# Lower recurrence levels as pinned 32x32 blocks, and another order of the first loads, in a two-layer hybrid decoder block

## The chip, the core and the metric

The kernel runs on one core of one Trainium2 chip. The metric is the device time of one execution in microseconds (us). Before the change it is 418.7 us, the median of three runs (418.44 to 418.85).

## What is computed

Two layers of a decoder trunk over 256 tokens of width 1024, in float32. Cut to what matters here:

```
for l in range(2):
    h = rms_norm(x)                       # 256 x 1024
    q_a,k_a,v_a, q_h,f_h,i_h, q_m, z = split(h @ w_in[l])   # 1024 x 5120
    o_a = moba_attention(rope(norm(q_a)), rope(norm(k_a)), v_a)   # 8 heads x 64, causal
    o_h = hgrn2(q_h, f_h, i_h)            # 4 heads x 128, gated linear recurrence
    k_m, v_m = split(rms_norm(mem) @ w_mem_kv[l])           # 1024 x 1024
    o_m = memory_attention(q_m, norm(k_m), v_m)             # 4 heads x 128
    x = x + (concat(o_a, o_h, o_m) * silu(z)) @ w_out[l]    # 1536 x 1024
```

The recurrence (`hgrn2`) has a decay between every two tokens t >= s that is a product of forget gates: score(t, s) = sum over d of q[t,d] * F[s+1..t, d] * k[s,d], and o = scores @ i.

## The kernel before

**The weight stream.** All weights come as 120 tiles of 128x1024 float32 (512 KB each), in one fixed order per layer: 8 of `w_mem_kv`, then the ten column groups of `w_in` (FH, QH, IH, KA, QA, ZH, ZA, ZM, QM, VA, four tiles each), then 12 of `w_out`. SyncE issues each tile's load into one of four buffers `wr`. ScalarE (ACT) rounds a tile to the matmul format, `wh` (L144, or L147 where the norm's gain is folded in, three buffers); VectorE (DVE) forms the rest `wl` = `wr` - `wh` (L156 or L159, three buffers). TensorE (PE) then makes three products for each part of the result (high by high, high by low, low by high), each collected in `acc`, four banks of PSUM. `group_kv`, `group_b` and `group_a` (L198 to L290) are these loops for the three layouts, `w_out_phase` (L1082) that of the output projection, where `part` issues the products of one weight tile and `both` those of the last two tiles for one quarter of the result; in layer 1 `both` is called with `pinned=True`.

**Side work.** Everything else is written as Python generators (`g_norm`, `g_mem_r`, `g_hgrn`, `g_qk`, `g_moba_unit` and others). After each half or whole weight tile, `slot` lets each active generator take one step (`step`); a `yield n` skips n - 1 turns. They use four further PSUM banks `sd` (`side_tile`, counted by `room` and `rel`). A scheduler then orders each engine's instructions; `tc.keep_in_program_order` pins an instruction behind the pinned one before it on the same engine. All matmuls but those go through `mm` (L196), which doesn't pin.

**The recurrence.** `g_hgrn` (L710 to L856) works on `Q`, `K`, `F` of 128 partitions (head dimension) by 8x128 columns (4 heads, two halves of the tokens), and fills the score tile `hST`. It goes through levels m = 0, 1, 2, 4, 8, 16, 32, 64: at level m, keys of the lower half of each run of 2m tokens meet queries of its upper half, and afterwards `Q` and `K` are multiplied by the gates `Tm` over m tokens.
- m = 0, 1, 2 are sums over partitions: a product `pr` on DVE, split into `prh` and `prl`, then a matmul by a matrix of ones for each (`column_sums`, five 512-column results per layer).
- m = 4, 8, 16 are eight products of 128x128 each in float32 (all pairs of a half), of which a mask `mk` keeps the right ones: two DVE `copy_predicated` into `hST` for each level (`keep`, L723).
- m = 32 and 64 are the needed blocks alone: sixteen 32x32 or eight 64x64 blocks, copied by ACT into `hST` (L812).
- The product between the two halves of the tokens (`xc`, four 128x128) and the outputs follow.

A matmul with float32 operands leaves two records in the trace (two passes), those of the weight stream one.

**The start.** SyncE's queue carries `gT`, the transposed `mem`, weight tiles 0 to 3, then both halves of `x` (`xs`, 512 KB each), then weight tiles 4 to 7, then `mem` (`memr`). `g_norm(0)` takes the squares of `x` on ACT (L387) and scales on DVE; `g_mem_r` squares `memr` on ACT (L370), pinned, once the first layer's `hT` is there.

Of the kernel before, what the change touches and what calls it, by code (L numbers as in the profile page):

```python
# [45 lines left out]
def hymba_kernel(ctx: ExitStack, tc: tile.TileContext, x, mem, mem_t, positions, w_in, w_out, w_mem_kv,  # L46
# [256 lines left out]
    for t in range(2):  # L303
        load(xs[:, t], dram(x, t * 128 * D, [[D, 128], [1, D]]))
    dma_to(8)
# [20 lines left out]
    onesf = sb.tile([128, 128], F32, name="onesf", tag="sg", bufs=2)  # L326
    nc.gpsimd.memset(onesf, 1.0)
    ones = cst.tile([128, 128], F32R, name="ones")
    nc.vector.tensor_copy(ones, onesf)
# [92 lines left out]
    mk = cst.tile([128, 7, 128], U8, name="mk")  # L422
# [7 lines left out]
    def g_setup():  # L430
# [56 lines left out]
        for l in range(DEPTH):  # L487
            for q in range(2):
# [4 lines left out]
                def gb(a, n):  # L493
# [11 lines left out]
        oi = small("oi", 1)  # L505
        nc.vector.tensor_scalar(oi.bitcast(I32), si, 1, None, op0=OP.bitwise_and)
        od = small("od", 1)
        nc.vector.tensor_copy(od, oi.bitcast(I32))
        ti = sb.tile([128, 128], I32, name="ti", tag="sg", bufs=2)
        nc.gpsimd.iota(ti, pattern=[[1, 128]], base=0, channel_multiplier=0)  # L510
        xi = sb.tile([128, 128], I32, name="xi", tag="sg", bufs=2)
        xf = sb.tile([128, 128], F32, name="xf", tag="sq", bufs=2)
        xu = sb.tile([128, 128], F32, name="xu", tag="sq", bufs=2)
        nc.vector.tensor_tensor(xi, ti, si.to_broadcast([128, 128]), op=OP.bitwise_xor)
        nc.gpsimd.tensor_copy(xf, xi)
        nc.gpsimd.affine_select(xu, xf, pattern=[[1, 128]], compare_op=OP.is_ge, fill=-1.0, base=0,
                                channel_multiplier=-1)
        yield
        for j, m in enumerate((0, 1, 2, None, 4, 8, 16)):
            if m is not None:  # L520
                nc.gpsimd.tensor_scalar(mk[:, j], xu, float(m), None, op0=OP.is_ge)  # L521
        nc.gpsimd.tensor_tensor(xu, xu, od.to_broadcast([128, 128]), op=OP.mult)
        nc.gpsimd.tensor_scalar(mk[:, 3], xu, 2.0, None, op0=OP.is_ge)
# [186 lines left out]
    def g_hgrn(l):  # L710
# [7 lines left out]
        def keep(g, j, cols=slice(0, 128)):  # L718
            view = St[:, :, cols]
            n = view.shape[2]  # L720
            per = 512 // n
            for b in range(len(g)):
                nc.vector.copy_predicated(view[:, b * per:(b + 1) * per],  # L723
                                          mk[:, j, cols][:, None, :].to_broadcast([128, per, n]),
                                          g[b].rearrange("p (a s) -> p a s", s=n))
            rel("sd", len(g))

        def column_sums(n, make):
            yield from take("P", "PTh", "PTl")
            pr = sb.tile([128, n], F32, name="pr", tag="P", bufs=2)  # L730
            prh = sb.tile([128, n], F32R, name="prh", tag="PTh", bufs=1)
            prl = sb.tile([128, n], F32R, name="prl", tag="PTl", bufs=1)
            make(pr)
            nc.scalar.copy(prh, pr)
            nc.vector.tensor_tensor(prl, pr, prh.bitcast(F32), op=OP.subtract)
            yield 2
            yield from room("sd", n // 512)
            for b in range(n // 512):
                o = side_tile()
                mm(o, ones, prh[:, b * 512:(b + 1) * 512], True, False)  # L740
                mm(o, ones, prl[:, b * 512:(b + 1) * 512], False, True)
                res.append(o)
            for w in ("P", "PTh", "PTl"):
                rel(w)
            yield
# [6 lines left out]
        while m < 128:  # L752
            yield 2
            res = []
# [4 lines left out]
            if m == 0:  # L759
                yield from column_sums(1024, lambda o: nc.vector.tensor_tensor(o, Q, K, op=OP.mult))  # L760
                nc.vector.tensor_tensor(Q, Q, F, op=OP.mult)
                keep(res, 0)
                m = 1
                continue
            if m == 1:
                yield from column_sums(512, lambda o: nc.vector.tensor_tensor(o, Qv[:, :, 1, 0], Kv[:, :, 0, 0],
                                                                              op=OP.mult))
            elif m == 2:

                def make(o):  # L770
                    for j in range(2):
                        nc.vector.tensor_tensor(o[:, j * 512:(j + 1) * 512].rearrange("p (n i) -> p n i", i=2),
                                                Qv[:, :, 1], Kv[:, :, 0, j:j + 1].to_broadcast([128, 256, 2]),
                                                op=OP.mult)
                yield from column_sums(1024, make)
            elif m < 32:
                yield from room("sd", 2)
                for b in range(2):
                    g = side_tile()
                    for i in range(4):  # L780
                        c = slice((b * 4 + i) * 128, (b * 4 + i + 1) * 128)
                        mm(g[:, i * 128:(i + 1) * 128], K[:, c], Q[:, c], True, True)
                    res.append(g)
            else:
                yield from room("sd", 1)
                g = side_tile()
                res.append(g)
                for i in range(8):
                    for q in range(0, 128, 2 * m):
                        c = i * 128 + q  # L790
                        mm(g[q:q + m, i * m:(i + 1) * m], K[:, c:c + m], Q[:, c + m:c + 2 * m], True, True)
            yield 2
            nc.vector.tensor_tensor(Qv[:, :, 1], Qv[:, :, 1], Tv[:, :, 0:1].to_broadcast([128, n, m]), op=OP.mult)
            nc.vector.tensor_tensor(Kv[:, :, 0], Kv[:, :, 0], Tv[:, :, 1:2].to_broadcast([128, n, m]), op=OP.mult)
            if m < 64:
                T2 = sb.tile([128, n], F32, name=f"hT{m}", tag=f"hT{m}", bufs=1)
                nc.vector.tensor_tensor(T2, Tv[:, :, 0], Tv[:, :, 1], op=OP.mult)
                Tm = T2
            if m == 1:
                keep(res, 1, slice(1, 128, 2))  # L800
            elif m == 2:
                for j in range(2):
                    nc.vector.copy_predicated(
                        St.rearrange("p a (n r) -> p a n r", r=4)[:, :, :, 2:4],
                        mk[:, 2 + j].rearrange("p (n r) -> p n r", r=4)[:, None, :, 2:4].to_broadcast([128, 8, 32, 2]),
                        res[j].rearrange("p (a n i) -> p a n i", a=8, i=2))
                rel("sd", 2)
            elif m < 32:
                keep(res, int(math.log2(m)) + 2)
            else:  # L810
                for q in range(0, 128, 2 * m):
                    nc.scalar.copy(St[q:q + m, :, q + m:q + 2 * m],  # L812
                                   res[0][q:q + m, 0:8 * m].rearrange("p (a s) -> p a s", s=m))
                rel()
            m *= 2
# [91 lines left out]
    def g_moba_unit(l, u):  # L907
# [9 lines left out]
        for t in range(2):  # L917
            nk = 128 * (t + 1)
            yield from room("sd", 2)
            ps = [side_tile() for _ in range(2)]  # L920
            for i in range(4):
                pi, e = divmod(i, 2)
                mm(ps[e][:, pi * nk:(pi + 1) * nk], qT[64 * e:64 * e + 64, 2 * u + pi, t * 128:(t + 1) * 128],
                   kT[64 * e:64 * e + 64, 2 * u + pi, 0:nk], True, True)
# [157 lines left out]
    def w_out_phase(l):  # L1082
# [64 lines left out]
    spawn(g_mem_r(), 6)  # L1147
# [64 lines left out]
```

## Time and profile before

| | us |
|---|---|
| median of three runs (range) | 418.7 (418.44 to 418.85) |
| the profiled execution | 418.65 |
| its span, first to last instruction | 416.9 |
| outside the span | 1.75 |
| PE busy | 410.4 |
| DVE busy | 327.9 |
| ACT busy | 256.7 |
| POOL (GpSimd) busy | 58.5 |

The profile is that of one execution. A timeline row gives the start and the length of a run of like instructions, engine, line, operation, result and operands, shape, and their count; brackets at its end give the engine's idle time just before and what ended it. PE's matmuls overlap (the next one starts before the last has ended), so what a matmul costs is the distance from its start to the start of the next.

### The profile page before, as it was taken

The page shows a single profiled execution, that of the slowest core. Times are in us where ns is not written, and L with a number is a line of the kernel's source. Part 1 is how long each engine was busy: PE and PEld are TensorE (multiplying, and loading weights), DVE is VectorE, ACT ScalarE, POOL GpSimd, SP SyncE. Part 2 cuts the span into 40 slices and gives each one's busy share as a digit, 9 for nine tenths or more (in the row PEclk, how much of TensorE's full clock was granted, in tenths as well). Part 3 has the DMA queues.
Part 4 walks back from the last instruction along what each step waited for, and adds up shares of the span by engine and source line. Part 5 has one row for each costly group of instructions (what it writes and reads, how often), then busy time and mean ns, then how long its engine had stood idle before and what let it go on. Part 6 is the DMA issues. An engine that isn't in the chain of part 4 may idle for free.

```text
span 416.9 us, 6337 instructions
## 1 busy us (share of the span) xinstructions
PE 410.4 (98%) x2288; PEld 344.9 (83%) x2288; DVE 327.9 (79%) x617; ACT 256.7 (62%) x419; POOL 58.5 (14%) x78
## 2 busy tenths in 40 slices
PE   8999999999999999999999999999999999999996
PEld 6788888888878888888878888888888898888885
DVE  4789799999788984695568689899978797646854
ACT  5868766544579766664357676644454994748440
POOL 2006309046000021000000020003130002100000
PEclk9999999999999999999999999999999999999999
DMA  7984565555441654354546555555444144641602
GB/s 256 413 298 149 162 198 162 163 182 169 138 144 61 200 154 151 102 151 130 173 151 204 171 183 174 180 175 167 162 153 153 58 145 151 204 151 50 201 5 101
DMA packets 19616, 67.68 MB, mean 162 GB/s; under 512 B 2432, under 2 KB 2816, under 8 KB 19584
## 3 DMA queue, kind: packets, MB, share of 16 engines
q1 hardware_dynamic: 19296, 67.12, 48.9%
q8 instruction: 18, 0.29, 0.3%
q10 hardware_dynamic: 288, 0.15, 0.1%
q14 instruction: 14, 0.11, 0.1%
HBM read 66.22 MB, written 1.05 MB: 161 GB/s over the span
## 4 chain that ended last, share of the span: by engine, by line
PE 88%; DVE 4%; DMA 3%; POOL 2%; ACT 1%; issue 1%; SPq 0%; DVEq 0%
PE acc L196 56%; PE acc L1096 15%; PE sd L196 12%; DMA wr<-in_w_mem_kv_dram 3%; PE sd L960 1%; DVE wl L156 1%; POOL mk L521 1%; PE sd L1059 1%; DVE wl L159 1%; PE sd L403 1%; PE sd L899 1%; ACT wh L147 1%; DVE xs L1130 0%; PE sd L698 0%; PE sd L1005 0%
## 5 line engine op out<-in xcount | busy, mean ns | idle before, releaser
L144 ACT CAST wh<-wr 128x1024 fp32r<-128x1024 f32 x104 | 109.0, 1051 | 84.0 <-PE acc L196 62.5
L156 DVE TENSOR_TENSOR wl<-wr,wh 128x1024 fp32r<-128x1024 f32 x104 | 126.8, 1223 | 32.8 <-ACT wh L144 32.2
L196 PE MATMUL acc<-wh,hT 128*128 128x512 f32 x384 | 123.0, 394 | 0.0
L196 PE MATMUL acc<-hT,wh 128*128 128x512 f32 x256 | 91.8, 399 | 0.2 <-DVE vml L593 0.2
L196 PEld LDWEIGHTS acc<-wh,hT 128*128 128x128 f32 x384 | 71.9, 188 | 14.5 <-ACT wh L144 0.4
L196 PE MATMUL acc<-wl,hT 128*128 128x512 f32 x192 | 76.3, 398 | 0.0
L196 PE MATMUL acc<-hT,wl 128*128 128x256 f32 x256 | 72.4, 283 | 0.1
L196 PEld LDWEIGHTS acc<-hT,wh 128*128 128x128 f32 x256 | 48.0, 188 | 12.5 <-ACT wh L144 0.7
L196 PEld LDWEIGHTS acc<-hT,wl 128*128 128x128 f32 x256 | 48.3, 189 | 0.7 <-DVE wl L156 0.4
L196 PEld LDWEIGHTS acc<-wl,hT 128*128 128x128 f32 x192 | 36.2, 188 | 6.6
L1096 PE MATMUL acc<-wh,yl 128*128 128x512 f32 (+1 forms) x96 | 36.1, 391 | 0.0
L1096 PE MATMUL acc<-wl,yh 128*128 128x512 f32 (+1 forms) x96 | 36.0, 390 | 0.0
L1096 PE MATMUL acc<-wh,yh 128*128 128x512 f32 (+1 forms) x96 | 35.5, 393 | 0.0
L196 PE MATMUL acc<-wh,mTh 128*128 128x512 f32 x64 | 25.5, 399 | 1.6 <-ACT wh L147 1.1
L159 DVE SCALAR_TENSOR_TENSOR wl<-wr,gT,wh 128x1024 fp32r<-128x1024 f32 (+1 forms) x17 | 20.2, 1219 | 8.3 <-ACT wh L147 8.1
L147 ACT ACTIVATE wh<-wr,gT 128x1024 fp32r<-128x1024 f32 (+1 forms) x17 | 18.4, 1100 | 11.9 <-PE acc L1096 4.8
L196 PE MATMUL acc<-wh,mTl 128*128 128x512 f32 x64 | 25.0, 390 | 0.0
L1096 PEld LDWEIGHTS acc<-wh,yl 128*128 128x128 f32 x96 | 18.1, 188 | 3.8
L1096 PEld LDWEIGHTS acc<-wl,yh 128*128 128x128 f32 x96 | 18.1, 188 | 3.7
L1096 PEld LDWEIGHTS acc<-wh,yh 128*128 128x128 f32 x96 | 18.1, 188 | 3.6
L196 PE MATMUL acc<-wl,mTh 128*128 128x512 f32 x64 | 20.8, 393 | 0.2 <-DVE wl L159 0.2
L196 PEld LDWEIGHTS sd<-hQ,hK 128*128 128x128 f32 (+2 forms) x208 | 17.5, 159 | 1.9 <-DVE mxa L929 0.5
(215 smaller groups left out, 630.2 us busy)
## 6 DMA issues: line engine op xcount, KB each, us to landing
wr<-in_w_in_dram SPq DMA_DIRECT2D x80, 512.0 KB, 3.3
wr<-in_w_out_dram SPq DMA_DIRECT2D x24, 512.0 KB, 3.4
wr<-in_w_mem_kv_dram SPq DMA_DIRECT2D x15, 512.0 KB, 3.9
xs<-in_x_dram SPq DMA_DIRECT2D x2, 512.0 KB, 8.9
memr<-in_mem_dram SPq DMA_DIRECT2D x2, 512.0 KB, 6.4
out_dram<-xs SPq DMA_DIRECT2D x3, 256.0 KB, 2.0
mraw<-in_mem_t_dram SPq DMA_DIRECT2D x2, 256.0 KB, 5.3
wr<-in_w_mem_kv_dram SPq DMA_DIRECT2D x2, 256.0 KB, 4.6
```

Source lines behind the costliest of these rows:

```text
L144: nc.scalar.copy(whs[i], raws[i])
L147: nc.scalar.activation(whs[i][:, sl], raws[i][:, sl], AF.Copy, scale=gT[:, g:g + 1])
L156: nc.vector.tensor_tensor(wls[i], raws[i], whs[i].bitcast(F32), op=OP.subtract)
L159: nc.vector.scalar_tensor_tensor(wls[i][:, sl], in0=raws[i][:, sl], scalar=gT[:, g:g + 1], in1=whs[i][:, sl].bitcast(F32), op0=OP.mult, op ...
L196: nc.tensor.matmul(o, lhsT=a, rhs=b, start=s, stop=e)
L403: ins = nc.tensor.transpose(pt[:, j * 256 + t * 128:j * 256 + (t + 1) * 128], xn[t][:, k * 128:(k + 1) * 128], ident)
L521: nc.gpsimd.tensor_scalar(mk[:, j], xu, float(m), None, op0=OP.is_ge)
L899: nc.tensor.transpose(pt[:, p * 128:(p + 1) * 128], kr[:, t, p * 128:(p + 1) * 128], ident)
L960: nc.tensor.transpose(pt[:, i * 128:(i + 1) * 128], P[:, i, bs], ident)
L1059: nc.tensor.transpose(pt[:, i * 256 + t * 128:i * 256 + (t + 1) * 128], P[:, t, i, b * 128:(b + 1) * 128], ident)
L1096: ins = nc.tensor.matmul(a, lhsT=y, rhs=wt[:, cs], start=n == (0 if to is None else nk - 2) and j == 0, stop=n == nk - 1 and j == 2)
```

## The change

**Recurrence.** Each of the levels 0, 1, 2, 4, 8, 16 becomes 32 products of 32x32 (8 groups i of 128 columns by 4 blocks j, j the inner loop), block j written to the partitions 32j to 32j+31 of one PSUM tile of 128x256. One masked DVE copy per level puts it into a compact tile `hSd` (128x8x32). After m = 16, four ACT copies put `hSd` on the diagonal blocks of `hST`. The column sums, the matrix of ones and the wide masks go; `mk` is 128x6x32. At m = 32 and 64 the blocks of two groups a and a+1 are written to different partitions of the result, and the ACT copies are four and two where they were two and one. All these matmuls go through the new `mm_row`, which pins them in program order on PE.

**Attention scores.** The products of `kT` and `qT` in `g_moba_unit` go through `mm_row` too, and there is a `yield` between the 128-wide ones and the 256-wide ones.

**Output projection.** `both` pins in layer 0 as well, so that the last two weight tiles finish one quarter of the result after another.

**Start.** The queue carries x's first half, weight tile 4 (the fifth), x's second half, weight tile 5 (the sixth), then 6, 7 and `mem`. `g_mem_r` waits for nothing, isn't pinned, and starts at the ninth slot.

```diff
+    def mm_row(o, a, b):
+        tc.keep_in_program_order(nc.tensor.matmul(o, lhsT=a, rhs=b, start=True, stop=True))
...
     for t in range(2):
         load(xs[:, t], dram(x, t * 128 * D, [[D, 128], [1, D]]))
+        dma_to(5 + t)
     dma_to(8)
...
     def g_mem_r():
-        while "hT0" not in done:
-            yield
         ss = small("ssm", 2)
         for t in range(2):
-            tc.keep_in_program_order(nc.scalar.activation(memr[t], memr[t], AF.Square, accum_out=ss[:, t:t + 1]))
+            nc.scalar.activation(memr[t], memr[t], AF.Square, accum_out=ss[:, t:t + 1])
...
-    mk = cst.tile([128, 7, 128], U8, name="mk")
+    mk = cst.tile([128, 6, 32], U8, name="mk")
+    hSd = cst.tile([128, 8, 32], F32, name="hSd")
...
         while m < 128:
             yield 2
-            res = []
+            yield from room("sd")
+            g = side_tile()
+            if m < 32:
+                for i in range(8):
+                    for j in range(4):
+                        c = slice(i * 128 + j * 32, i * 128 + j * 32 + 32)
+                        mm_row(g[j * 32:j * 32 + 32, i * 32:i * 32 + 32], K[:, c], Q[:, c])
+            else:
+                for a in range(0, 8, 2):
+                    for q in range(0, 128, 2 * m):
+                        for b in range(2):
+                            c = (a + b) * 128 + q
+                            mm_row(g[q + b * m:q + b * m + m, a // 2 * m:(a // 2 + 1) * m],
+                                   K[:, c:c + m], Q[:, c + m:c + 2 * m])
+            yield 2
...
-            elif m < 32:
-                yield from room("sd", 2)
-                for b in range(2):
-                    g = side_tile()
-                    for i in range(4):
-                        c = slice((b * 4 + i) * 128, (b * 4 + i + 1) * 128)
-                        mm(g[:, i * 128:(i + 1) * 128], K[:, c], Q[:, c], True, True)
-                    res.append(g)
...
+            if m < 32:
+                j = m.bit_length()
+                nc.vector.copy_predicated(hSd, mk[:, j][:, None, :].to_broadcast([128, 8, 32]),
+                                          g[:, 0:256].rearrange("p (a s) -> p a s", s=32))
...
+            if m == 16:
+                for q in range(0, 128, 32):
+                    nc.scalar.copy(hST.rearrange("p h t s -> p (h t) s")[q:q + 32, :, q:q + 32], hSd[q:q + 32])
+            m = 2 * m or 1
...
         for t in range(2):
             nk = 128 * (t + 1)
+            if t:
+                yield
             yield from room("sd", 2)
...
-                both(t, c, 0, 256 if split else 512, last)
+                both(t, c, 0, 256 if split else 512, True)
...
-    spawn(g_mem_r(), 6)
+    spawn(g_mem_r(), 9)
```

The first place where it moves instructions is PE in layer 0, at the recurrence's level m = 16 (`sd<-hQ,hK`; `acc` rows are the weight stream). Before:

```order
L196 MATMUL acc<-hT,wh 128x512
L196 MATMUL acc<-hT,wl 128x256
L196 MATMUL sd<-hQ,hK 128x128 x8
L196 MATMUL acc<-hT,wh 128x512
L196 MATMUL acc<-hT,wl 128x256
```

After (L200 is `mm_row`, L851 transposes the attention's keys `kr`):

```order
L196 MATMUL acc<-wl,hT 128x512
L196 MATMUL acc<-wh,hT 128x512 x2
L200 MATMUL sd<-hQ,hK 32x32 x32
L851 MATMUL sd<-ident,kr 128x128 x4
L196 MATMUL acc<-wl,hT 128x512
L196 MATMUL acc<-wh,hT 128x512 x2
```

Eight wide products have become 32 small ones, and the level has moved to an earlier weight group, right ahead of four transposes. The other five low levels look alike, each one burst of 32 with 20 to 31 matmuls of the weight stream between two of them.

The second place is PE in layer 0 at the first unit's 256-wide attention scores (`sd<-kT,qT`). Before:

```order
L196 MATMUL acc<-hT,wh 128x512
L196 MATMUL acc<-hT,wl 128x256
L196 MATMUL sd<-kT,qT 128x256 x4
L196 MATMUL acc<-hT,wh 128x512
L196 MATMUL acc<-hT,wl 128x256
```

After:

```order
L196 MATMUL acc<-hT,wl 128x256
L200 MATMUL sd<-kT,qT 128x256
L196 MATMUL acc<-hT,wh 128x512
L196 MATMUL acc<-hT,wl 128x256
L196 MATMUL acc<-hT,wh 128x512
L200 MATMUL sd<-kT,qT 128x256 x3
L196 MATMUL acc<-hT,wl 128x256
```

One of the four now stands alone, with three matmuls of the weight stream between it and the other three; in layer 1 it is the same.

The third place is ACT at the start of the program, where it makes `wh` of the first tiles, squares `x` (`xn`) and later `mem` (`memr`). Before:

```order
L147 ACTIVATE wh<-wr,gT 128x1024
L387 ACTIVATE xn,ssx<-xs 128x1024 x2
L147 ACTIVATE wh<-wr,gT 128x1024 x4
L411 ACTIVATE hT<-sd,gT 128x256 x5
L144 CAST wh<-wr 128x1024
```

After:

```order
L147 ACTIVATE wh<-wr,gT 128x1024
L386 ACTIVATE xn,ssx<-xs 128x1024
L147 ACTIVATE wh<-wr,gT 128x1024
L386 ACTIVATE xn,ssx<-xs 128x1024
L147 ACTIVATE wh<-wr,gT 128x1024 x3
L369 ACTIVATE memr,ssm<-memr 128x1024
L410 ACTIVATE hT<-sd,gT 128x256 x3
L369 ACTIVATE memr,ssm<-memr 128x1024
```

The fifth tile's `wh` now stands between the two squares of `x`, and the squares of `mem` come earlier. ACT also loads its function tables fifteen times where it did so eleven times, twice more in each layer.

More of the change, by code (lines that the diff above doesn't have):

```diff
@@ L325, in hymba_kernel @@
     make_identity(nc, ident)
[L326 to L329, printed above, removed]
     pw = cst.tile([128, 16], F32, name="pw")
@@ L504, in g_setup @@
                                 base=0, channel_multiplier=1)
[L505 to L514, printed above, removed]
+        nc.gpsimd.memset(hSd, 0.0)
+        sp = small("sp", 1)
+        nc.vector.tensor_scalar(sp.bitcast(I32), si, 31, None, op0=OP.bitwise_and)
+        ti = sb.tile([128, 32], I32, name="ti", tag="sg", bufs=2)
+        nc.gpsimd.iota(ti, pattern=[[1, 32]], base=0, channel_multiplier=0)
+        xi = sb.tile([128, 32], I32, name="xi", tag="sg", bufs=2)
+        xf = sb.tile([128, 32], F32, name="xf", tag="sq", bufs=2)
+        ge = sb.tile([128, 32], F32, name="ge", tag="sq", bufs=2)
+        nc.vector.tensor_tensor(xi, ti, sp.bitcast(I32).to_broadcast([128, 32]), op=OP.bitwise_xor)
         nc.gpsimd.tensor_copy(xf, xi)
-        nc.gpsimd.affine_select(xu, xf, pattern=[[1, 128]], compare_op=OP.is_ge, fill=-1.0, base=0,
-                                channel_multiplier=-1)
+        nc.vector.tensor_tensor(xi, ti, sp.bitcast(I32).to_broadcast([128, 32]), op=OP.subtract)
+        nc.gpsimd.tensor_copy(ge, xi)
         yield
[L519 to L523, printed above, removed]
+        nc.gpsimd.tensor_scalar(ge, ge, 0.0, None, op0=OP.is_ge)
+        nc.gpsimd.tensor_scalar(xf, xf, 1.0, None, op0=OP.add)
+        nc.gpsimd.tensor_tensor(xf, xf, ge, op=OP.mult)
+        for j, m in enumerate((0, 1, 2, 4, 8, 16)):
+            nc.gpsimd.tensor_scalar(mk[:, j], xf, float(m + 1), None, op0=OP.is_ge)
     setup = g_setup()
@@ L716, in g_hgrn @@
         St = hST.rearrange("p h t s -> p (h t) s")
[L718 to L745, printed above, removed]
         Tm = F
@@ L758, in g_hgrn @@
                 Tv = Tm.rearrange("p (n two) -> p n two", two=2)
-            if m == 0:
-                yield from column_sums(1024, lambda o: nc.vector.tensor_tensor(o, Q, K, op=OP.mult))
-                nc.vector.tensor_tensor(Q, Q, F, op=OP.mult)
[L762 to L775, printed above, removed]
-            elif m < 32:
-                yield from room("sd", 2)
-                for b in range(2):
-                    g = side_tile()
-                    for i in range(4):
-                        c = slice((b * 4 + i) * 128, (b * 4 + i + 1) * 128)
-                        mm(g[:, i * 128:(i + 1) * 128], K[:, c], Q[:, c], True, True)
-                    res.append(g)
-            else:
[L785 to L810, printed above, removed]
-                for q in range(0, 128, 2 * m):
-                    nc.scalar.copy(St[q:q + m, :, q + m:q + 2 * m],
-                                   res[0][q:q + m, 0:8 * m].rearrange("p (a s) -> p a s", s=m))
-                rel()
@@ L815, in g_hgrn @@
-            m *= 2
+                nc.vector.tensor_tensor(Qv[:, :, 1], Qv[:, :, 1], Tv[:, :, 0:1].to_broadcast([128, n, m]), op=OP.mult)
+                nc.vector.tensor_tensor(Kv[:, :, 0], Kv[:, :, 0], Tv[:, :, 1:2].to_broadcast([128, n, m]), op=OP.mult)
+                if m < 64:
+                    T2 = sb.tile([128, n], F32, name=f"hT{m}", tag=f"hT{m}", bufs=1)
+                    nc.vector.tensor_tensor(T2, Tv[:, :, 0], Tv[:, :, 1], op=OP.mult)
+                    Tm = T2
+            else:
+                nc.vector.tensor_tensor(Q, Q, F, op=OP.mult)
@@ new lines, in g_hgrn @@
+            if m < 32:
+                j = m.bit_length()
+                nc.vector.copy_predicated(hSd, mk[:, j][:, None, :].to_broadcast([128, 8, 32]),
+                                          g[:, 0:256].rearrange("p (a s) -> p a s", s=32))
+            else:
+                S2 = hST.rearrange("p h t s -> p (h t) s").rearrange("p (a b) s -> p a b s", b=2)
+                for q in range(0, 128, 2 * m):
+                    for b in range(2):
+                        nc.scalar.copy(S2[q:q + m, :, b, q + m:q + 2 * m],
+                                       g[q + b * m:q + b * m + m, 0:4 * m].rearrange("p (a s) -> p a s", s=m))
@@ L816, in g_hgrn @@
+            rel()
+            if m == 16:
+                for q in range(0, 128, 32):
+                    nc.scalar.copy(hST.rearrange("p h t s -> p (h t) s")[q:q + 32, :, q:q + 32], hSd[q:q + 32])
+            m = 2 * m or 1
         yield 3
@@ L921, in g_moba_unit @@
             for i in range(4):
-                pi, e = divmod(i, 2)
-                mm(ps[e][:, pi * nk:(pi + 1) * nk], qT[64 * e:64 * e + 64, 2 * u + pi, t * 128:(t + 1) * 128],
-                   kT[64 * e:64 * e + 64, 2 * u + pi, 0:nk], True, True)
+                pi, e = i // 2, i % 2
+                mm_row(ps[e][:, pi * nk:(pi + 1) * nk], qT[64 * e:64 * e + 64, 2 * u + pi, t * 128:(t + 1) * 128],
+                       kT[64 * e:64 * e + 64, 2 * u + pi, 0:nk])
             yield
```

## The prediction

> **What bounds the kernel now.** I read the page first, for the shares and the chain.
>
> ```profile
> span 416.9 us, 6337 instructions
> PE 410.4 (98%) x2288; PEld 344.9 (83%) x2288; DVE 327.9 (79%) x617; ACT 256.7 (62%) x419; POOL 58.5 (14%) x78
> PE 88%; DVE 4%; DMA 3%; POOL 2%; ACT 1%; issue 1%; SPq 0%; DVEq 0%
> GB/s 256 413 298 149 162 198 162 163 182 169 138 144 61 200 154 151 102 151 130 173 151 204 171 183 174 180 175 167 162 153 153 58 145 151 204 151 50 201 5 101
> ```
>
> TensorE is busy for 410.4 of 416.9 us and carries 88% of the chain that ended last. A cut on another engine is worth what it takes from a PE wait; a cut on PE is worth its whole length. Next I looked for a stage in which another engine is as full, among the tables of busy time by window (length, then sum and count for PE, PEld, DVE, ACT and POOL, then clock, DMA share and GB/s).
>
> ```profile
> 80.00:100.00 20.00, 20.00 (x104) 16.84 (x103) 20.00 (x38) 8.71 (x12) 6.48 (x4) 1.00 0.52 169
> ```
>
> In the recurrence's first levels DVE is full too, but PE is never idle there, so DVE isn't ahead of it. The change is thus to be costed by starts of PE's matmuls: in the timeline of PE I take the distance between the starts of the two `acc` matmuls around a piece of side work, less what that distance is without it.
>
> **The low levels, removed.** Timeline of PE around level m = 16, around an undisturbed stretch, and around two column sums of one 512-column result:
>
> ```profile
> 108.30 0.28 PE L196 MATMUL acc<-hT,wl 128*128 128x256 f32 x1
> 108.42 1.95 PE L196 MATMUL sd<-hQ,hK 128*128 128x128 f32 x16
> 110.12 0.47 PE L196 MATMUL acc<-hT,wh 128*128 128x512 f32 x1
> 110.43 0.28 PE L196 MATMUL acc<-hT,wl 128*128 128x256 f32 x1
> ...
> 117.52 0.40 PE L196 MATMUL acc<-hT,wh 128*128 128x512 f32 x1
> 117.75 0.28 PE L196 MATMUL acc<-hT,wl 128*128 128x256 f32 x1
> 117.87 0.39 PE L196 MATMUL acc<-hT,wh 128*128 128x512 f32 x1
> 118.19 0.70 PE L196 MATMUL sd<-hQ,hK 128*32 128x32 f32 x32
> 118.82 0.39 PE L196 MATMUL acc<-hT,wl 128*128 128x256 f32 x1
> 119.04 0.40 PE L196 MATMUL acc<-hT,wh 128*128 128x512 f32 x1
> ...
> 66.99 0.62 PE L196 MATMUL sd<-prh,ones 128*128 128x512 f32 x2
> 67.44 0.39 PE L196 MATMUL acc<-wl,hT 128*128 128x512 f32 x1
> ```
>
> A 512-wide matmul costs 0.23 (117.52 to 117.75), a 256-wide one 0.12 (117.75 to 117.87), the pair 0.35. Level 16 takes 2.13 (108.30 to 110.43) where the pair alone takes 0.35: 1.78 for eight products. By the code there are three such levels: 5.34 per layer. A column sum costs 0.45 / 2 = 0.225, and there are ten: 2.25 per layer. Removed: 7.59.
>
> **The low levels, added.** No row shows 32x32 blocks in four column groups, but m = 32 has them in two. Sixteen passes of 128 columns take 1.70 (108.42 to 110.12), 0.106 each, so 32 columns stream in 0.0266. Level m = 32 costs 1.17 (117.87 to 119.04) less 0.35 = 0.82. One after another its 32 passes would stream for 0.85, yet only 0.63 lies between 118.19 and 118.82: blocks written to different partitions overlap. With two at a time that is 16 slots of 0.0266 = 0.43, and 0.39 for getting into and out of the small form. The new level has 64 passes; its inner loop goes through four partition groups, so four at a time make 16 slots too: 0.82, six times 4.92. Bounds: with all entries and exits shared with the transposes beside them, 0.43 each; two at a time or one at a time are rivals below. I take 0.82, the row with the same number of slots.
>
> The Trainium skill, "TensorEngine Tiling (Array Packing)", section "Tiling Modes", lists four independent tiles for 128 rows by 32 columns and says that switching the mode drains the engine. The 0.39 agrees with the second; no run here shows four yet. Against the change speaks "TensorE: Matmul & The Clock Gate", section "Wait — 56ns, not 53.3ns?": starts come no closer than some 25 ns however small a matmul is, so 64 passes would take 1.60, an estimate, where my sum has 0.43. The row at 118.19 speaks against it: 32 passes in 0.63 are 19.7 ns each.
>
> **Levels 32 and 64, and the attention scores.**
>
> ```profile
> 126.41 0.40 PE L196 MATMUL acc<-hT,wh 128*128 128x512 f32 x1
> 128.04 0.39 PE L196 MATMUL acc<-hT,wh 128*128 128x512 f32 x1
> ...
> 115.10 0.28 PE L196 MATMUL acc<-hT,wl 128*128 128x256 f32 x1
> 116.71 0.28 PE L196 MATMUL acc<-hT,wl 128*128 128x256 f32 x1
> ```
>
> At m = 32 four groups now alternate instead of two: 8 slots, 0.21 + 0.39 = 0.60, saving 0.22. At m = 64, 1.63 - 0.35 = 1.28 is 16 passes one after another (16 x 0.053 = 0.85) and 0.43; two groups halve the first part: saving 0.42. The four 256-wide score products cost 1.61 - 0.35 = 1.26: eight passes would stream 8 x 0.2125 = 1.70, so they overlap in pairs (0.85) with 0.41 around. Of the first unit's four, one now stands alone and three follow: three pairs' time becomes two for the three, one for the single, so 0.42 more of streaming and a second entry of 0.41 to 0.42: 0.84 lost per layer. Between 0, if the single one hides, and 0.84 I take all, since no row shows such a matmul hidden.
>
> Per layer: 4.92 - 0.22 - 0.42 + 0.84 - 7.59 = -2.47; two layers **-4.94**. Bursts that now stand beside transposes may share an entry, 0.2 to 0.4 per layer more; that stays in the range.
>
> **The start.** Timelines of PE, ACT and DVE:
>
> ```profile
> 16.61 1.07 PE L196 MATMUL acc<-wl,mTh 128*128 128x512 f32 x4
> 18.00 0.50 PE L196 MATMUL acc<-wh,mTh 128*128 128x512 f32 x1 [0.31 <-ACT wh L147]
> 18.33 0.40 PE L196 MATMUL acc<-wh,mTl 128*128 128x512 f32 x1
> 19.71 0.39 PE L196 MATMUL acc<-wh,mTl 128*128 128x512 f32 x1
> 20.29 0.50 PE L196 MATMUL acc<-wl,mTh 128*128 128x512 f32 x1 [0.19 <-DVE wl L159]
> ```
>
> ```profile
> 12.95 1.15 ACT L147 ACTIVATE wh<-wr,gT 128x1024 fp32r<-128x1024 f32 x1 [0.22 <-DMA wr<-in_w_mem_kv_dram]
> 15.43 1.06 ACT L387 ACTIVATE xn<-xs 128x1024 f32<-128x1024 f32 x1
> 16.79 4.99 ACT L147 ACTIVATE wh<-wr,gT 128x1024 fp32r<-128x1024 f32 x4 [0.21 <-DVE msx L391]
> ```
>
> ```profile
> 18.96 4.87 DVE L159 SCALAR_TENSOR_TENSOR wl<-wr,gT,wh 128x1024 fp32r<-128x1024 f32 x4
> ```
>
> PE waits twice for the fifth tile. The four matmuls at 16.61 would end at 16.61 + 4 x 0.23 = 17.53 but the next starts at 18.00: 0.47, and it takes 0.33 instead of 0.23 after the pause: 0.10. At 19.71 + 0.23 = 19.94 the next should come and comes at 20.29: 0.35, and 0.10 more behind it. Together 1.02. The cause is the queue: at 413 GB/s (the page's second slice) 512 KB land every 1.27, tile 3 was used on landing at 12.95, and two halves of x lie between it and tile 4: 12.95 + 3 x 1.27 = 16.76, and ACT takes it at 16.79. With one half ahead it lands at 15.49, and its `wh` is ready 1.1 to 1.2 later, before 17.53. What is late next is x's second half and so tile 5's `wl` on DVE, behind the scaling of x: from x's square at 15.43 to that `wl` group at 18.96 are 3.53; from 16.76 they give 20.29, and 1.22 for one `wl` (4.87 / 4) gives 21.5. From 17.53 PE has twelve matmuls of tile 4 and eight of tile 5 with `wh` to do first, 20 x 0.23, so it is wanted at 22.1: 0.6 to spare. I take **-1.02**, between 0 (the pause moves to tile 5) and that.
>
> ```profile
> 36.85 0.28 PE L196 MATMUL acc<-hT,wl 128*128 128x256 f32 x1
> 37.37 0.50 PE L196 MATMUL acc<-hT,wh 128*128 128x512 f32 x1 [0.25 <-DVE vml L593]
> ...
> 210.55 0.40 PE L1096 MATMUL acc<-wh,yl 128*128 128x512 f32 x1
> 211.45 0.48 PE L196 MATMUL acc<-wh,mTh 128*128 128x512 f32 x1 [0.51 <-DVE xs L1130]
> 211.76 0.40 PE L196 MATMUL acc<-wh,mTl 128*128 128x512 f32 x1
> ```
>
> At 36.85 + 0.12 PE waits 0.40 for `vml` to free a bank, and pays 0.10 behind it. `mem`'s squares, on which `vml`'s factor hangs, now come before `hT`. Between 0 and 0.50 I take **-0.3**, since other DVE work stands in between as well.
>
> **Between the layers.** All four `acc` banks of the output projection end together, so the next layer's first matmul waits for their addition into `xs`: 211.45 - 210.55 - 0.23 = 0.67, and 211.76 - 211.45 - 0.23 = 0.08 behind it. Pinned, the quarters end one after another, each 1.4 (six matmuls of 0.23) before the next, and the first three additions are done by the end: **-0.75**. If the last addition were still waited for, 0.
>
> **New waits.** ACT gets two more table loads per layer and three more copies.
>
> ```profile
> 121.69 1.28 ACT L941 ACT_TABLE_LOAD   x1
> 133.19 1.05 ACT L144 CAST wh<-wr 128x1024 fp32r<-128x1024 f32 x1
> ...
> 135.66 0.48 PE L196 MATMUL acc<-hT,wh 128*128 128x512 f32 x1
> ```
>
> Two loads are 2.56 per layer. Queued behind them on ACT is the next `wh`, and PE waits for that. Where ACT's lead is shortest, `wh` is done at 133.19 + 1.05 = 134.24 and used at 135.66: 1.4 to spare. Both loads in one such place cost 2.56 - 1.4 = 1.14 per layer, spread out nothing; I take 0.4, nearer to nothing as one load fits into the lead: **+0.8** for both layers.
>
> **DVE.** One of the masked copies that go:
>
> ```profile
> L723 DVE COPY_PREDICATED hST<-mk,sd 128x512 f32<-128x512 uint8 x18 | 14.1, 796 | 0.0
> ```
>
> DVE loses 14.1 us of these, and the column sums' products, for six copies of half the width per layer. I cost that at zero: PE hides it, as the 80 to 100 us window shows. It is also why pinned levels should not wait: the update of Q and K between two levels had two such copies beside it and now has one of half the size.
>
> **Sum.** -4.94 - 1.02 - 0.3 - 0.75 + 0.8 = -6.2 against the profiled 418.65 (416.9 and 1.75 outside), which stands 0.05 under the median: **412.4 us**.
>
> **Rivals.** *Two at a time.* PE runs only pairs, as in all the rows: a level has 32 slots, between 32 x 0.0266 + 0.39 = 1.24 and twice 0.63 plus the remaining 0.19 = 1.45; at 1.33, six are 7.98, m = 32 saves nothing, and a layer comes to 7.98 - 0.42 + 0.84 - 7.59 = +0.81. With the other terms (-1.27) that is +0.35: 419.0. For it: pairs are all that is shown. Against: nothing shows a limit at two. Chance 0.12.
>
> *One at a time, slower.* The new level's blocks write all of a PSUM tile's partitions in turn and don't overlap at all: 64 x 0.0266 + 0.39 = 2.09, six 12.54, m = 32 and m = 64 as before, +0.84 - 7.59: +5.8 per layer, so 418.65 + 11.6 - 1.3 = 429. It decides once a level costs more than 1.23, where 6 x 1.23 + 0.84 - 7.59 eats the other terms' 0.64 per layer. Against it stands the row at 118.19. Chance 0.04. The skill's 25 ns would make a level 1.99 and the time near 428, an estimate; it is counted here.
>
> *New waits eat a part.* Table loads at their full 1.14 or more per layer, or a pinned level that waits for DVE while the weight stream stands behind it (20 to 31 matmuls, 4.6 to 7.1 us, lie between two levels): 1.5 to 4 more, 414 to 416.5. For it: the DVE window is full, and a pinned matmul can't be passed by a later pinned one. Chance 0.14.
>
> **How the numbers follow.** My forecast, 409.8 to 414 (shared entries -1.6, the unknown terms +1.6), has 0.68; the waits 0.14; two at a time 0.12; one at a time 0.04; 0.02 is left for faster still. The range 409.8 to 416.8 holds the first two. About 0.2%, 0.84 us, is what a measurement of this kernel can tell from no change: faster has the first, the waits and the rest with part of two at a time, 0.86; within it lies most of two at a time, 0.08; slower 0.06.
>
> **What would show it.** Right: level bursts of 64 records with 0.6 to 0.7 us between the start of the first and the next `acc` matmul; no pause at 17.5 and 20 us; a first matmul of layer 1 without a wait for `xs`. Wrong: bursts of 1.2 (pairs) or 2 us (single file), a lone `kT` matmul costing nothing, new brackets on PE naming ACT `wh` or DVE `hQ`.

## The result, and the profile after

| | before | after |
|---|---|---|
| median, us | 418.66 | 411.12 (410.86 to 411.35) |
| the profiled execution's span | 416.9 | 409.6 |
| PE busy | 410.4 | 404.7 |
| DVE busy | 327.9 | 305.6 |
| ACT busy | 256.7 | 261.7 |

The ratio after to before is 0.9816, 95% interval 0.9802 to 0.9831: 7.5 us faster, where 6.2 was forecast. The page of the changed kernel:

```profile
span 409.6 us, 7613 instructions
PE 404.7 (99%) x2940; PEld 336.7 (82%) x2940; DVE 305.6 (75%) x592; ACT 261.7 (64%) x431; POOL 54.5 (13%) x79
PE 97%; DMA 1%; DVE 0%; SPq 0%; ACT 0%; issue 0%; DVEq 0%
```

PE's share of the chain has gone from 88% to 97%: almost no wait for another engine is left in it. PE's busy time fell by 5.7 and the span by 7.3; the other 1.6 is time in which PE stood idle before. Part of a wait counts as busy (the pause before 18.00 us in the kernel before is 0.47 by the starts and 0.31 in its bracket), so the distances of starts, below, give the better split.

**A low level.** Timeline of PE around the first one in layer 0 (start, length, instruction):

```profile
61.67 0.39 PE L196 MATMUL acc<-wh,hT 128*128 128x512 f32 x1
61.98 0.76 PE L200 MATMUL sd<-hQ,hK 128*32 128x32 f32 x64
62.68 0.51 PE L196 MATMUL acc<-wh,hT 128*128 128x512 f32 x1
63.02 0.39 PE L196 MATMUL acc<-wl,hT 128*128 128x512 f32 x1
```

From 61.67 to 63.02 are 1.35, less two undisturbed 512-wide matmuls (0.46): the level costs 0.89; 0.82 was forecast. The 64 passes take 0.70 from first start to the next `acc`, 10.9 ns each. In the single records of this burst the first starts of a round through the four groups lie 6 or 7 ns apart, and a whole round takes 32 ns.

**Level 64 and the attention scores.** The same view further on:

```profile
109.87 0.69 PE L200 MATMUL sd<-hQ,hK 128*64 128x64 f32 x16
110.49 0.71 PE L200 MATMUL sd<-kT,qT 64*128 64x128 f32 x8
...
113.33 0.28 PE L196 MATMUL acc<-hT,wl 128*128 128x256 f32 x1
113.54 0.70 PE L200 MATMUL sd<-kT,qT 64*128 64x256 f32 x2
114.16 0.50 PE L196 MATMUL acc<-hT,wh 128*128 128x512 f32 x1
114.50 0.28 PE L196 MATMUL acc<-hT,wl 128*128 128x256 f32 x1
114.61 0.40 PE L196 MATMUL acc<-hT,wh 128*128 128x512 f32 x1
114.94 1.13 PE L200 MATMUL sd<-kT,qT 64*128 64x256 f32 x6
116.00 0.38 PE L196 MATMUL acc<-hT,wl 128*128 128x256 f32 x1
116.22 0.40 PE L196 MATMUL acc<-hT,wh 128*128 128x512 f32 x1
```

Level 64 takes 0.62 from its start to that of the scores and has no exit of its own, where before the whole level cost 1.28. The lone 256-wide score costs 114.50 - 113.33 - 0.35 = 0.82 (two records: one matmul), the other three 116.22 - 114.61 - 0.35 = 1.26: together 0.82 more than the four in one piece before.

**The start and the seam.** Timeline of PE at the start, and where layer 1's first matmuls on `hT` begin:

```profile
16.88 1.07 PE L196 MATMUL acc<-wl,mTh 128*128 128x512 f32 x4
17.79 0.39 PE L196 MATMUL acc<-wh,mTh 128*128 128x512 f32 x1
...
19.60 1.07 PE L196 MATMUL acc<-wl,mTh 128*128 128x512 f32 x4
20.51 0.39 PE L196 MATMUL acc<-wh,mTh 128*128 128x512 f32 x1
...
22.32 0.62 PE L196 MATMUL acc<-wl,mTh 128*128 128x512 f32 x2
...
229.79 0.39 PE L196 MATMUL acc<-wl,mTh 128*128 128x512 f32 x1
230.17 0.50 PE L196 MATMUL acc<-hT,wh 128*128 128x512 f32 x1
230.50 0.28 PE L196 MATMUL acc<-hT,wl 128*128 128x256 f32 x1
```

From 16.88 to 22.32 there are 24 matmuls, and each start follows the one before it by the undisturbed distance: 24 x 0.227 = 5.44. Neither pause is left. The wait between the layers has gone as well, but a new one of 230.17 - 229.79 - 0.23 = 0.15, and 0.10 behind it, stands at 230.

**Where the 7.3 us went.** I took the prediction's measure (starts of `acc` matmuls, less their undisturbed distance) over both whole traces. Side work on PE falls from 73.4 to 68.6: 4.84. Waits between two `acc` matmuls fall by 2.4, of which 2.3 can be named: at the start 1.03, for `vml` 0.51, near 52 and 64 us in layer 0 0.35 and 0.23, between the layers 0.75; against them 0.32 new at 7 us and 0.26 at 230. The first `acc` matmul started 0.11 earlier.

### The profile page after: what moved, and what is told of

Same layout as the page of the kernel before. It is cut to its first block, busy times and chain, and to the rows that moved or that the text cites. A ratio compares the mean times of both kernels' runs of the same rounds, so it can differ in the third digit from the quotient of the medians.

```text
span 409.6 us, 7613 instructions
## 1 busy us (share of the span) xinstructions
PE 404.7 (99%) x2940; PEld 336.7 (82%) x2940; DVE 305.6 (75%) x592; ACT 261.7 (64%) x431; POOL 54.5 (13%) x79
## 4 chain that ended last, share of the span: by engine, by line
PE 97%; DMA 1%; DVE 0%; SPq 0%; ACT 0%; issue 0%; DVEq 0%
PE acc L196 65%; PE acc L1050 16%; PE sd L196 6%; PE sd L200 4%; DMA wr<-in_w_mem_kv_dram 1%; PE sd L914 1%; PE sd L851 1%; PE sd L1013 1%; PE sd L402 1%; PE sd L698 0%; PE sd L959 0%; PE sd L578 0%; SPq L119 0%; ACT wh L147 0%; DVE xs L1084 0%; DVE xs L1091 0%
## 5 line engine op out<-in xcount | busy, mean ns | idle before, releaser
L1050 PE MATMUL acc<-wl,yh 128*128 128x512 f32 (+1 forms) x96 | 37.4, 389 | 0.0
L1050 PE MATMUL acc<-wh,yl 128*128 128x512 f32 (+1 forms) x96 | 37.1, 393 | 0.0
L1050 PE MATMUL acc<-wh,yh 128*128 128x512 f32 (+1 forms) x96 | 36.6, 392 | 0.0
L819 POOL TENSOR_TENSOR rka<-msa,pw 128x8 f32<-128x8 f32 x4 | 14.2, 3560 | 54.2 <-DVE msa L818 54.2
```

The costliest lines, as they stand in the source:

```text
L819: nc.gpsimd.tensor_tensor(r[:, t8], ms[:, t8], pw[:, :8], op=OP.pow)
L1050: ins = nc.tensor.matmul(a, lhsT=y, rhs=wt[:, cs], start=n == (0 if to is None else nk - 2) and j == 0, stop=n == nk - 1 and j == 2)
```

## The experiments

Times below are compared through the ratio to the kernel before, run in turn on the same chip (its median was 419.05 to 419.34 there).

**Single file.** Only the two loops change places:

```diff
-                for i in range(8):
-                    for j in range(4):
+                for j in range(4):
+                    for i in range(8):
```

> The changed kernel with the two loops of a low level swapped (block j outer, group i inner), so that eight blocks in a row go to the same partitions. Theory (blocks overlap because neighbours go to different column groups): 64 passes one after another at 31.6 ns, the spacing of the pairs at m = 32, are 2.02 us and 0.33 around them, 2.35 instead of the 0.89 that the changed kernel's bursts cost; 12 levels make +17.5, 428 to 430. Rival (the order within a burst doesn't matter, the gain comes from the fewer columns and from DVE's relief): 411 to 412. A floor of 25 ns from start to start whatever the group: 64 x 25 = 1.60 and 0.33, +12.5, near 424.

**Pairs.** The groups alternate in twos:

```diff
-                for i in range(8):
-                    for j in range(4):
+                for i, j in [(i, j + e) for j in (0, 2) for i in range(8) for e in range(2)]:
```

> The changed kernel with the low levels' blocks going through two partition groups at a time, first 0 and 1, then 2 and 3. Theory (as many overlap as there are groups in turn): 32 slots of 31.6 ns are 1.01, with 0.33 around 1.34 instead of 0.89; 12 levels +5.4, 416 to 417. Rival one (the engine overlaps two at most): no change from the changed kernel, 411. Rival two (order doesn't matter): 411 too; the single-file run tells these two apart.

Measured: 426.39, ratio 1.0178 (1.0155 to 1.0201), and 415.85, ratio 0.9927 (0.9905 to 0.9949). The same 32 products in another order turn a gain of 1.8% into a loss of 1.8%. Timeline of PE around one level, single file and then pairs:

```profile
72.42 0.39 PE L196 MATMUL acc<-wh,hT 128*128 128x512 f32 x1
72.74 1.91 PE L200 MATMUL sd<-hQ,hK 128*32 128x32 f32 x64
74.58 0.50 PE L196 MATMUL acc<-wh,hT 128*128 128x512 f32 x1
74.91 0.39 PE L196 MATMUL acc<-wl,hT 128*128 128x512 f32 x1
```

```profile
61.65 0.39 PE L196 MATMUL acc<-wh,hT 128*128 128x512 f32 x1
61.97 1.11 PE L200 MATMUL sd<-hQ,hK 128*32 128x32 f32 x64
63.01 0.50 PE L196 MATMUL acc<-wh,hT 128*128 128x512 f32 x1
63.34 0.39 PE L196 MATMUL acc<-wl,hT 128*128 128x512 f32 x1
```

A level costs 74.91 - 72.42 - 0.46 = 2.03 in single file, 63.34 - 61.65 - 0.46 = 1.23 in pairs and 0.89 in fours. The prediction's rivals had priced the first two at 2.09 and 1.33 (1.24 at the least). The expectation for single file, 2.35 at 31.6 ns a pass, was 0.32 too high for a level. In the single records 41 of the 63 distances in such a burst are 31 or 32 ns, as it took, but around each of the three changes of group some passes start 5 or 6 ns after the one before, which brings the mean down to (2.03 - 0.33) / 64 = 26.6. Over twelve levels that is 3.8 us; the time came out only some 2 us lower than expected, and the difference isn't traced. The number of column groups in turn sets the price, and two isn't the limit.

**Recurrence and score pins alone**, the start's loads, mem's squares and the output projection as before.

```diff
-        dma_to(5 + t)
-                both(t, c, 0, 256 if split else 512, True)
+                both(t, c, 0, 256 if split else 512, last)
-    spawn(g_mem_r(), 9)
+    spawn(g_mem_r(), 6)
```

(and `g_mem_r` waits for `hT0` and pins its squares again.)

> The changed kernel without its start order, with mem's squares as before and without the pinned quarters in layer 0: the recurrence and the attention pins alone. Theory (PE's side work is 4.84 us shorter in the changed kernel, and two waits of 0.35 and 0.23 in layer 0 that the prediction didn't count went with DVE's relief): 418.7 - 5.4 = 413.3, with the pauses at 17 and 20 us, the one for the bank of vml and the one between the layers still there. Rival (most of the gain is DVE's relief, the start and the seam): 416 or more.

**The rest alone**: the kernel before with the lines above as in the change.

```diff
+        dma_to(5 + t)
-                both(t, c, 0, 256 if split else 512, last)
+                both(t, c, 0, 256 if split else 512, True)
-    spawn(g_mem_r(), 6)
+    spawn(g_mem_r(), 9)
```

> The kernel before with the new start order, mem's squares as in the change and the pinned quarters in layer 0, and the old recurrence and attention. Theory (terms add): start -0.7 to -1.0, vml -0.5, seam -0.75: 416.4 to 416.8. Rival (the pauses only move, as DVE is as full as before): 418 or more.

Measured: 413.74, ratio 0.9871 (0.9856 to 0.9886), or 5.4 us, and 416.3, ratio 0.9939 (0.9917 to 0.9962), or 2.6. They add up to 8.0 where the change has 7.7 by its ratio, which agrees within the intervals. The parts aren't quite independent: the two waits near 52 and 64 us, 0.58 together, are gone from either run's trace and so stand in both numbers. The waits of PE in the first:

```profile
PE acc L196 <- DVE xs L1085: 0.5, 1, 0.5
PE acc L196 <- DVE vml L594: 0.3, 1, 0.3
```

The waits for `xs` between the layers and for `vml` are still there although DVE is as light as in the changed kernel, so DVE's relief didn't take them. Of the two pauses at the start, which were expected here too, this execution has only the second (0.26, and 0.11 behind it). Its first `acc` matmul starts at 6.99 us, where the kernel before has 6.51. With the old order of loads the two pauses come to 1.02, 0.37 and 1.26 in the three traces that have it (before, this run, the seam alone), so one execution doesn't fix what they cost.

**Seam alone**, the kernel before with `both(..., True)`.

```diff
-                both(t, c, 0, 256 if split else 512, last)
+                both(t, c, 0, 256 if split else 512, True)
```

> The kernel before with the last two weight tiles of layer 0's output projection pinned quarter by quarter, nothing else. Theory: the wait of 0.67 and the 0.08 behind it between the layers go, 418.7 - 0.75 = 417.9. Rival (the wait moves to the next tiles' wh or wl, whose buffers the last two tiles now hold to the end): 418.5 or more.

**Start alone**, the kernel before with the new order of loads.

```diff
         load(xs[:, t], dram(x, t * 128 * D, [[D, 128], [1, D]]))
+        dma_to(5 + t)
```

> The kernel before with the new order of the first loads, nothing else. Theory: both pauses for the fifth tile go, 418.7 - 1.0 = 417.7. Rival (the pause moves to tile six, whose wl stands behind x's scaling on DVE): 418.4 or more, with a new bracket near 21 us.

Measured: 418.46, ratio 0.9983 (0.9974 to 0.9991), 0.7 us or 0.4 to 1.1; and 417.0, ratio 0.9952 (0.994 to 0.9964), 2.0 us. The start is worth twice what I gave it. PE's waits in that run:

```profile
PE sd L196 <- DVE dm L319: 1.0, 1, 1.0
PE acc L196 <- ACT wh L147: 1.0, 1, 1.0
PE acc L196 <- DVE xs L1131: 0.5, 1, 0.5
```

What is left of waits are the very first matmuls (`dm`, `wh`) and the seam. The wait for `vml` has gone too, with mem's squares untouched, and so have the two near 52 and 64 us: with the pauses, 1.02 + 0.51 + 0.58 = 2.1, which is the measured gain. Of the last two the first shows in the kernel before as a distance:

```profile
52.25 0.39 PE L196 MATMUL acc<-hT,wh 128*128 128x512 f32 x1
52.72 0.39 PE L196 MATMUL acc<-hT,wl 128*128 128x256 f32 x1
```

52.25 to 52.72 is 0.47 where 0.23 is undisturbed. The row has no bracket naming what ended it. The recurrence-only run shows neither of the two distances either, so each part alone takes them away; which wait they were stays open.

**Mem's squares as before**, in the changed kernel.

```diff
+        while "hT0" not in done:
+            yield
-            nc.scalar.activation(memr[t], memr[t], AF.Square, accum_out=ss[:, t:t + 1])
+            tc.keep_in_program_order(nc.scalar.activation(memr[t], memr[t], AF.Square, accum_out=ss[:, t:t + 1]))
-    spawn(g_mem_r(), 9)
+    spawn(g_mem_r(), 6)
```

> The changed kernel with mem's squares as before (pinned on ACT, behind the first layer's hT, sixth slot). The prediction's step: the earlier squares free the bank that vml holds, so the wait of 0.40 and 0.10 behind it comes back near 37 us: 411.1 + 0.5 = 411.6. Rival (the start order alone took that wait away, since the kernel before with only the start order showed none of it): 411.1, no bracket naming vml.

Measured: 412.2, ratio 0.9842 (0.9825 to 0.986). PE's waits:

```profile
PE sd L196 <- DVE dm L323: 1.0, 1, 1.0
PE acc L196 <- ACT wh L147: 0.8, 1, 0.8
```

No wait for `vml` comes back. The ratio lies 0.3% above that of the change, with overlapping intervals; if that is a difference, it isn't this wait.

**Scores as before**, in the changed kernel.

```diff
-            if t:
-                yield
-                mm_row(ps[e][:, pi * nk:(pi + 1) * nk], qT[64 * e:64 * e + 64, 2 * u + pi, t * 128:(t + 1) * 128],
-                       kT[64 * e:64 * e + 64, 2 * u + pi, 0:nk])
+                mm(ps[e][:, pi * nk:(pi + 1) * nk], qT[64 * e:64 * e + 64, 2 * u + pi, t * 128:(t + 1) * 128],
+                   kT[64 * e:64 * e + 64, 2 * u + pi, 0:nk], True, True)
```

> The changed kernel with the attention scores as before: not pinned, no turn between the 128-wide and the 256-wide ones. The prediction priced pin and turn as a loss of 0.84 per layer. If that holds against this kernel too: 411.1 - 1.6 = 409.5. Rival (they avert something worse: in this kernel's order the unpinned 256-wide scores of both units stand two and two, both of one row group, which can't overlap): each half is four passes of 0.2125 and 0.41 around, 1.26, so 2.52 for a unit; first unit +0.44, second +1.26 per layer, 411.1 + 3.4 = 414.5.

Measured: 416.14, ratio 0.9943 (0.9921 to 0.9966): 1.3% above the change's ratio, some 5 us. Timeline of PE at the first unit's 256-wide scores:

```profile
114.01 0.28 PE L196 MATMUL acc<-hT,wl 128*128 128x256 f32 x1
114.22 1.13 PE L196 MATMUL sd<-kT,qT 64*128 64x256 f32 x4
115.61 0.28 PE L196 MATMUL acc<-hT,wl 128*128 128x256 f32 x1
```

Two matmuls (four records) cost 115.61 - 114.01 - 0.35 = 1.25, as much as four that alternate: both use the same row group (the same 64 of PE's 128 rows). A second such pair follows at 117.09, and the second unit is split likewise. From level 32 to the outputs' last matmul the side work costs 12.36 where the changed kernel's costs 10.68, so 3.4 for both layers, the rival's price. All side work is 4.6 longer; the remaining 1.2 has, among others, a wait for `wl` of 0.4 in each layer. So in the changed kernel's order pin and turn are a gain; against the kernel before, whose four stood together, they are a loss of 0.82, where the prediction gave 0.84.

**Scores whole**, first unit's 256-wide and the second unit later.

```diff
+        if u:
+            yield 2
...
             if t:
-                yield
+                yield 3 if u == 0 else 1
```

> The changed kernel with the first unit's 256-wide scores two turns later and the second unit two turns later, so that all four stand together in both units (beside the product between the halves and beside the outputs' first matmuls). Theory (a split costs an entry and the overlap, 0.82 per layer in the changed kernel's trace): 411.1 - 1.6 = 409.5. Rival (the later scores make softmax and its transposes late, and PE waits there, or nothing changes as the split is paid elsewhere): 411 or more.

Measured: 416.61, ratio 0.9938 (0.9925 to 0.9951), 5 us slower than the change. Timelines of ACT and PE:

```profile
137.24 0.49 ACT L897 ACTIVATE P<-P,nba,rq 128x128 f32<-128x128 f32 x1
...
141.42 0.19 ACT L897 ACTIVATION_READ_ACCUMULATOR P<-P,nba,rq 128x1 f32 x1
141.51 1.04 ACT L144 CAST wh<-wr 128x1024 fp32r<-128x1024 f32 x1
```

```profile
143.01 0.71 PE L196 MATMUL acc<-wh,hT 128*128 128x512 f32 x2
144.99 0.50 PE L196 MATMUL acc<-wl,hT 128*128 128x512 f32 x1 [1.27 <-DVE wl L156]
```

All scores stand whole, and the 0.82 per layer is there on PE. But eight exponentials of the second unit now stand in one piece on ACT (137.24 to 141.51) ahead of the next `wh`; its `wl` comes after, and PE waits 1.27, in both layers. These waits, with what stands behind them, are 3.1 of the 5 us. Later transposes and value products fall apart into more pieces: side work as a whole is 1.6 longer, although the scores are 1.6 shorter. This is the prediction's "new waits" rival, in an order in which it bites.

**Two milder orders.** One turn less before the first unit's wide scores and one more before the second's; and the first unit's as in the run above, with the second unit not delayed as a whole.

```diff
+        if u:
+            yield 2
...
             if t:
-                yield
+                yield 2
```

> The changed kernel with both units' 256-wide scores one turn later than in it and the second unit two turns later: all scores whole, as in the run with two turns, but three of the first unit's exponentials have a tile's wh between them and the rest on ACT. Theory (whole scores are worth 1.6 us, and what cost more there was wh behind the exponentials): with that wait away 409.5. Rival (the second unit's softmax is late in any case, and PE waits for a weight tile behind its exponentials): 411 or more, with a bracket of 1 us or so naming DVE wl or ACT wh near 143 us.

```diff
             if t:
-                yield
+                yield 3 if u == 0 else 2
```

> The changed kernel with the first unit's 256-wide scores two turns later (whole, beside the product between the halves) and the second unit's one turn later; of the second unit's 128-wide scores one then stands in that same burst and three apart. Theory (bursts alone): -0.82 for the whole scores, +0.2 for the one apart, per layer: 411.1 - 1.2 = 409.9. Rival (later scores, exponentials ahead of wh): 411 or more.

Measured: 411.83, ratio 0.9832 (0.9815 to 0.9848), and 411.7, ratio 0.9819 (0.9806 to 0.9833): neither can be told from the change. In the first, PE's timeline shows part of what gave the gain back, here in layer 0 and once more in layer 1:

```profile
145.03 0.38 PE L916 MATMUL sd<-ident,P 128*128 128x128 f32 x2
145.91 0.50 PE L196 MATMUL acc<-wl,hT 128*128 128x512 f32 x1 [0.50 <-DVE wl L156]
```

**Exponentials pinned**, on top of the first of these two.

```diff
-                nc.scalar.copy(whs[i], raws[i])
+                tc.keep_in_program_order(nc.scalar.copy(whs[i], raws[i]))
...
-                nc.scalar.activation(P[:, i, kc[t]], P[:, i, kc[t]], AF.Exp, bias=nb[:, c:c + 1],
-                                     scale=rq[:, r:r + 1], accum_out=sm[:, c:c + 1])
+                tc.keep_in_program_order(nc.scalar.activation(P[:, i, kc[t]], P[:, i, kc[t]], AF.Exp, bias=nb[:, c:c + 1],
+                                     scale=rq[:, r:r + 1], accum_out=sm[:, c:c + 1]))
```

(the gain-folding cast of `wh` is pinned likewise.)

> The kernel of the shorter whole scores with ACT's casts to wh and the attention's exponentials pinned in the order in which they are written, so that no more than four exponentials stand ahead of a wh; ACT then loads its tables seven times instead of fifteen. Theory (what whole scores gained was given back where wh stood behind eight exponentials): the wait for wl near 145 us goes; on PE alone the bursts are about 0.8 shorter than the changed kernel's: 0.2% below it, a ratio to the kernel before of 0.980. Rival (a pinned wh now stands behind exponentials that wait for their row maxima, and the weight stream stops): 412 or more, a ratio of 0.984 or more, with brackets naming ACT wh or DVE wl between 125 and 145 us.

Measured: 421.18, ratio 1.0047 (1.0033 to 1.0061). Both missed the place. Timelines of ACT and PE, and the busy time by window (columns as in the prediction's window row):

```profile
46.18 1.28 ACT L484 ACT_TABLE_LOAD   x1
49.97 0.23 ACT L484 ACTIVATE sc<-rt 128x32 f32<-128x32 f32 x1 [2.50 <-DVE rt L483]
50.10 2.92 ACT L144 CAST wh<-wr 128x1024 fp32r<-128x1024 f32 x3
```

```profile
51.19 0.79 PE L196 MATMUL acc<-hT,wh 128*128 128x512 f32 x1 [5.89 <-ACT wh L144]
...
162.39 0.50 PE L196 MATMUL acc<-wl,hT 128*128 128x512 f32 x1 [0.48 <-DVE wl L156]
```

```profile
40.00:44.00 4.00, 4.00 (x25) 3.52 (x24) 2.90 (x12) 2.87 (x6) 3.77 (x10) 1.00 0.39 132
...
51.19:55.30 4.11, 3.95 (x11) 2.95 (x12) 3.61 (x3) 1.84 (x2) 4.11 (x8) 0.50 0.41 135
```

Pinning moved three `wh` behind the sine of the position angles (L484), which waits for DVE; PE stood still for 5.89 us and then ran at half the clock for about 4. The wait that the pins were meant to remove is there too, later and in both layers (162.39): eight exponentials again stand in one piece on ACT (154.82 to 159.09) ahead of the next `wh`, not four. So what whole scores gain without that wait stays open.

## Why the prediction was right

Step by step, in us of the whole kernel:

- *Recurrence and scores*, -4.94 forecast, -4.84 measured on PE. The levels run four at a time, as taken, and the row of level 32 was the right one to price them by: 0.89 for 0.82. The split of that price was off: 16 rounds take 0.56 from the first start, not 0.43, and entry and exit 0.33, not 0.39. The close total is partly luck. Ten levels that stand alone cost 0.7 more than forecast, and levels 16, 32 and 64, beside transposes and scores, 0.6 less, as the shared exits in the range allowed. The lone score cost 0.82 per layer for 0.84.
- *The start*, -1.02 forecast: both pauses went (1.03), and tile 5's `wl` was in time. The old order's pauses differ between executions, as said above, so the closeness is that of one trace with another. The changed kernel's execution has a wait of 0.32 at 7 us, before any of this; it isn't in the run with the start alone.
- *The bank of `vml`*, -0.3 forecast, -0.51 measured, and here the reason was wrong: mem's earlier squares aren't needed for it. The start order alone takes the wait away, and putting the squares back doesn't bring it back.
- *Two waits not counted*, 0.58 together, near 52 and 64 us. They carry no bracket; the list of what PE waits for doesn't show them, the distances of starts do. I had read the list.
- *Between the layers*, -0.75 forecast and seen, with 0.26 given back at 230. Every kernel with pinned quarters shows that wait, those without don't. What it is for wasn't tried; in the changed kernel it ends 0.05 after ACT's copy of `kn` out of `acc` (229.53, 0.59 long), which would fit a wait for that bank.
- *New waits*, +0.8 forecast: none came. This term is most of the 1.3 us between 412.4 and 411.1, with the uncounted waits behind it. The scores-whole run shows that the mechanism is real (1.27 per layer), with eight exponentials in one piece ahead of a `wh`. Eight alone aren't enough: the kernel before has eight from 122.99 to 127.25 with a `wh` right behind, and PE doesn't wait. The term's count of ACT's work was also short: the pages give ACT 431 instructions for 419, and with four table loads more that makes four more copies per layer, not three.

The rivals' times, by the runs that made them, are 415.85 for pairs and 426.39 for single file, where the prediction gave 419.0 and 429. In both, 1.3 of the difference are the other terms (2.6 in the run of the rest alone, 1.27 in the prediction); a level in pairs cost 1.23 for 1.33 (1.2 over twelve), one in single file 2.03 for 2.09 (0.7); about 0.6 in each is left over.

Against the change stood the floor of 25 ns between starts (the Trainium skill, "TensorE: Matmul & The Clock Gate", section "Wait — 56ns, not 53.3ns?"). The traces contradict it for neighbours in different column groups: 10.9 ns a pass on the average, 6 or 7 between neighbours. Within one group starts lie 31 or 32 ns apart, above the floor, so these runs don't show whether there is one.

## What to carry to other kernels

Small products are cheap where neighbours in program order go to different column groups, and the loop order decides it: the same 32 products cost 0.89, 1.23 or 2.03. Price a new form by the row with the same number of slots, and look for waits by the distances between starts, not by the list of waits alone. Where work on PE is made shorter or later, the next question is what then stands in one piece ahead of the weight cast on ACT. Whether the recurrence's small products need their pins wasn't tried: every run with them has both the pins and the new form.

## What was not expected of the hardware

- In all three orders a round takes about the same time: 31 or 32 ns for one pass of 32 columns in one group, for one pass in each of two groups, and at first for one in each of four. On the average, with entry and exit taken off, it is 26.6 ns in single file, (1.23 - 0.33) / 32 = 28 in pairs and (0.89 - 0.33) / 16 = 35 in fours, because passes overlap around a change of group and the later rounds of four are less even. So the gain from two to four is 1.6 times, not two.
- Two fp32 matmuls of the same row group cost as much as four that alternate: 1.25 and 1.26.
- After 5.89 us without a matmul PE's granted clock was 0.50 over the next 4.1 us (1.00 from 40 to 44 us), so by an estimate from these two figures, half of 4.1, the wait cost some 2 us more than its own length.
